# Relative bias: low parts added in DRAM and onto the mask by the transfers, instead of by GpSimd

## The chip, the cores and the metric

The kernel runs on one core of one Trainium2 chip. The metric is the device time of one execution in microseconds, the median of three runs.

## What is computed

The program runs two transformer blocks one after the other on one sequence of 256 tokens, D = 1024, all in float32 accuracy: multi-head latent attention (MLA), a squared-ReLU MLP, MoBA attention, a second MLP, then a gated delta rule mixer and a forgetting-attention mixer. The part that the change touches is the bias of MoBA. With 256 tokens there is a single block of keys, so MoBA is plain causal attention with a T5-style relative bias:

```python
def rel_bias(pq, pk):
    return table_h[h_i4, t5_bucket(pq - pk)].astype(jnp.float32)
...
lg_own = (jnp.einsum('bhqd,bhtd->bhqt', qi, k_own).astype(jnp.float32) * scale
          + rel_bias(pq4, pos_own[:, None, None, :]))
causal = (own * MOBA_BLOCK + t_ids)[None, :] <= q_idx[:, None]
parts.append(jnp.where(causal, lg_own, -jnp.inf))
```

For each of 8 heads, 256 queries and up to 256 keys the bias is one of 32 table entries, chosen by the distance of the two positions.

## The kernel before

Every projection is made of three matmuls in a reduced format (`mm3`, L171 to L173): high part times high part and the two cross products. A weight tile of 512 KB is loaded by SP into a ring of four (`load_w`, L161), ScalarE copies its high part (L164, ring of four), and VectorE, in a few places GpSimd (called POOL in the profile), subtracts to get the low part (L165, ring of four). The order of instructions on each engine is worked out before the run by a planner that follows the program's order as priority and a cost for each instruction; on the chip each engine's queue runs in that fixed order and waits on semaphores.

The bias is built beside the first MLP. `rel_bias_setup` makes the differences of neighbouring table rows as a high and a low part, side by side in one weight tile `tw` of 64 columns: rows 0 to 31 of a result come from the high parts, rows 32 to 63 from the low parts. In each of the MLP's 16 steps `rel_bias_step` multiplies `tw` with masks of "position difference reaches bucket n", and ScalarE copies the result into a staging tile `stg` (L413), which alternates between two buffers. After every second step, eight times in all, POOL issues eight transfers of 64 KB each that write the staging tile to a DRAM tensor `bias_d` (L418): four carry the high parts to `bias_d[0]`, four the low parts to `bias_d[1]`. After the MLP `rel_bias_finish` reads both halves back into SBUF with the query on the partitions: the high halves into `bias` (L422, L423), the low halves into two tiles `b2` of four heads each (L427, L428); POOL adds `b2` (L429) and then the causal mask `cmask` (L430), four tensor operations of 128x1536.

`bias` lies in the first 3072 columns of tile `bias_s`; the positions lie behind it in the same tile. It is first read in MoBA's attention, where VectorE adds it to the scaled logits (`attend`, L339). Before that MoBA norms its input: `ms_eps` and `rsqrt` (L182 to L187), a Newton iteration of small VectorE operations, and the query, key and value projections for four heads (`qkv_quad`, with `head_sumsq`, L698, and `proj_tok`).

In MLA, `rope_apply` (L476 to L479) rotates the queries of each pair of heads on POOL; the last pair's last instruction is the addition at L479. `queued(list)` makes the instructions traced inside it follow the given ones in the order of their engine.

Of the kernel before, what the change touches and what calls it, by code (L numbers as in the profile page):

```python
# [19 lines left out]
P = 128  # L20
S = 256
# [89 lines left out]
def kernel(ctx: ExitStack, tc: tile.TileContext, I: dict, out: bass.AP, small_at: dict):  # L111
# [12 lines left out]
    def slot(i, shape, dt=F32):  # L124

        return big.tile(shape, dt, tag=f"s{i}", name=f"s{i}")
# [13 lines left out]
    @contextmanager  # L140
    def queued(after):

        with ExitStack() as es:
            for i in after or ():
                es.enter_context(tc.issue_after(i))
            yield
# [131 lines left out]
    def wview(name, l=None):  # L278
        w = I[name] if l is None else I[name][l]
        return w.rearrange("(k p) n -> p k n", p=P)  # L280
# [15 lines left out]
    def out_proj(oT, w, then, between=None):  # L296

        a = [[acc_tile() for _ in range(2)] for _ in range(NT)]  # L300
        wc = []

        def group(t, ks):
            for k in ks:
                for hf in range(2):
                    mm3(a[t][hf], sl(oT, slice(None), k, slice(t * P, (t + 1) * P)),
                        sl(wc[k], slice(None), slice(hf * 512, (hf + 1) * 512)), k == 0, k == KD - 1)

        for k in range(4):
            wc += load_w(w[:, k:k + 1, :], 1, D)  # L310
            if between is None:
                for t in range(NT):
                    group(t, (k,))
            else:
                group(0, (k,))
        if between is not None:
            between()
            group(1, range(4))
        for k in range(4, KD):
            wc += load_w(w[:, k:k + 1, :], 1, D)  # L320
        for t in range(NT):
            group(t, range(4, KD))
            for hf in range(2):
                then(t, hf, a[t][hf])
# [42 lines left out]


    bias = bias_s[:, 0:3072].rearrange("p (h k) -> p h k", h=H)
    bias_d = dr.tile([2, S, H, S], F32, tag="bias_d", name="bias_d")  # L370

    def rel_bias_setup():
        pk = bias_s[:, 3072:3328]
# [23 lines left out]
    def rel_bias_step(i, pq, pk, tw):  # L397

        b, half = divmod(i, 2)
        if i == 0:  # L400
            rel["masks"] = slot(12, [P, 8, S], F32R)
            masks(0, pq, pk)
        if i < 15:
            masks(i + 1, pq, pk)
        if half == 0:
            rel["stg"] = slot(9 + b % 2, [64, 8, S])
        stg = rel["stg"]
        for g2 in (2 * half, 2 * half + 1):
            p = aux_tile()
            for j in range(2):  # L410
                T.matmul(p[0:64, j * S:(j + 1) * S], lhsT=tw[:, 0, :], rhs=rel["masks"][:, (4 * i + 2 * (g2 % 2) + j) % 8],
                         start=True, stop=True)
            A.activation(stg[:, 2 * g2:2 * g2 + 2, :], p[0:64].rearrange("p (a b) -> p a b", a=2), AF.Copy)  # L413
        if half == 1:
            for part in range(2):
                for q4 in range(4):
                    r0 = part * 32 + q4 * 8
                    nc.gpsimd.dma_start(  # L418
                        bias_d[part, 64 * q4 + 8 * b:64 * q4 + 8 * b + 8].rearrange("g h k -> h g k"), stg[r0:r0 + 8])

    def rel_bias_finish():
        nc.gpsimd.dma_start(bias[:, :, 0:128], bias_d[0, 0:128, :, 0:128])  # L422
        nc.gpsimd.dma_start(bias[:, :, 128:384], bias_d[0, 128:256])  # L423
        for h4 in range(2):
            hs = slice(4 * h4, 4 * h4 + 4)
            b2 = slot(13 + h4, [P, 4, 384])
            nc.gpsimd.dma_start(b2[:, :, 0:128], bias_d[1, 0:128, hs, 0:128])  # L427
            nc.gpsimd.dma_start(b2[:, :, 128:384], bias_d[1, 128:256, hs])  # L428
            G.tensor_tensor(bias[:, hs], bias[:, hs], b2, op=ALU.add)  # L429
            G.tensor_tensor(bias[:, hs], bias[:, hs], cmask[:, None, :].to_broadcast([P, 4, 384]), op=ALU.add)  # L430


    def rope_tables():
# [37 lines left out]
    def rope_apply(eng, dst, src, tab, nh):  # L471

        ta, tb = tab
        sh = [P, NT, nh, 32]
        t2 = w1k([P, NT, nh, ROPE])
        eng.tensor_tensor(t2[:, :, :, 0:32], src[:, :, :, 32:64], tb[:, :, None, 0:32].to_broadcast(sh), op=ALU.mult)  # L476
        eng.tensor_tensor(t2[:, :, :, 32:64], src[:, :, :, 0:32], tb[:, :, None, 32:64].to_broadcast(sh), op=ALU.mult)
        eng.tensor_tensor(dst, src, ta[:, :, None, :].to_broadcast([P, NT, nh, ROPE]), op=ALU.mult)
        eng.tensor_tensor(dst, dst, t2, op=ALU.add)  # L479

    def mla():
        hT = pair_tile(1, KD)
# [72 lines left out]
        kT = slot(6, [P, H, S])  # L555
        vt = slot(7, [P, NT, H, P])
        oT = pair_tile(3, H)
        wkv_c = []

        def heads(hp):  # L560
            wc = load_w(wq[:, :, hp * 384:(hp + 1) * 384], 3, 384, (G,) if hp == 0 else None)
# [36 lines left out]
            for dst, c0, i in ((qn, 0, 0), (kn, 192, 2)):  # L598
                V.tensor_tensor(dst, raw[:, :, :, c0:c0 + P], r6[:, :, i, :, None].to_broadcast([P, NT, 2, P]), op=ALU.mult)
            qr = w1k([P, NT, 2, ROPE])  # L600
            rope_apply(G, qr, raw[:, :, :, 128:192], tabs["q"], 2)
            V.tensor_tensor(qr, qr, r6[:, :, 1, :, None].to_broadcast([P, NT, 2, ROPE]), op=ALU.mult)
            for src, dst, g in ((qn, qT, gs[:, 0:1]), (kn, kT, gs[:, 3:4])):
                p = aux_tile()
# [23 lines left out]
        for stage, hp in ((heads, 0), (attention, 0), (heads, 1), (attention, 1), (heads, 2), (attention, 2), (heads, 3), (attention, 3)):  # L628
            stage(hp)
        out_proj(oT, wview("mla_w_o", 0), add_x)  # L630


    def mlp(l, extra=None):
# [626 lines left out]
        post_norm_out(oT, wview("fox_w_out_2", 0), "fox_post_norm_2", store)  # L1260


    mla()
    rb = rel_bias_setup()
    mlp(0, lambda f: rel_bias_step(f, *rb))
    rel_bias_finish()
# [28 lines left out]
```

## Time and profile before

| | |
|---|---|
| median of three runs | 982.36 us (981.1 to 984.11) |
| the profiled execution's own time | 988.49 us |
| its span, first to last instruction | 986.7 us |
| mean granted TensorE clock in it | 0.967 |
| HBM read, written | 147.84 MB, 5.78 MB |

The profile is one execution of its own. PE is TensorE's matmul side, PEld its weight loads, DVE is VectorE, ACT is ScalarE, POOL is GpSimd, SP the engine that only issues transfers. The tile names are those of the program, with `s` for any of the large numbered slots, so `bias`, `stg` and `b2` all read as `s`. PEclk is the granted TensorE clock as a share of the full one.

### The profile page before, as it was taken

The numbers are of one execution on the slowest core, as the hardware profiler recorded it, in microseconds if no ns is written. First come the engines' busy times: TensorE is split into PE (matmuls) and PEld (weight loads), VectorE is DVE, ScalarE is ACT, GpSimd is POOL, SyncE is SP. The second block draws the span as 40 slices with busy tenths as digits, with TensorE's granted clock in tenths as the row PEclk, the third lists the DMA queues.
The fourth block names the chain that finished last, engine by engine and source line by source line (L and its number), as shares of the span: only waits on it lengthen the run. The fifth ranks groups of instructions, "written<-read, shape, count | busy, mean of one in ns | idle before, by whom it ended". The sixth has DMA issues, their size and how long they took to land.

```text
span 986.7 us, 14702 instructions
## 1 busy us (share of the span) xinstructions
PE 911.0 (92%) x5474; PEld 790.9 (80%) x5474; DVE 649.1 (66%) x1331; ACT 519.9 (53%) x963; POOL 171.9 (17%) x205
## 2 busy tenths in 40 slices
PE   8799889999999979998999999999993897999996
PEld 8576689998988768778999989889992885789884
DVE  6897375655555875756555445678982578877775
ACT  6675354645445535645454445578652124856653
POOL 1420121111112710022000000010396303000000
PEclk9899999999999979999999999999997898999998
DMA  8344147666667645436566655355753104365431
GB/s 286 112 152 129 44 135 228 193 192 192 192 192 226 201 150 162 140 106 204 179 190 196 196 180 171 117 168 157 211 155 91 33 22 149 96 227 171 140 117 65
DMA packets 92456, 154.61 MB, mean 157 GB/s; under 512 B 9160, under 2 KB 60128, under 8 KB 92128
## 3 DMA queue, kind: packets, MB, share of 16 engines
q1 hardware_dynamic: 87072, 141.53, 45.9%
q0 software_dynamic: 5168, 12.10, 4.4%
q8 instruction: 43, 0.70, 0.3%
q14 instruction: 29, 0.24, 0.1%
q10 hardware_dynamic: 144, 0.03, 0.0%
HBM read 147.84 MB, written 5.78 MB: 156 GB/s over the span
## 4 chain that ended last, share of the span: by engine, by line
PE 40%; DMA 18%; DVE 17%; ACT 10%; issue 8%; POOL 6%; DVEq 0%; ACTq 0%; SPq 0%; POOLq 0%
DMA raw<-in_mlp_w_in_dram 14%; PE acc L171 9%; PE acc L173 9%; PE acc L172 9%; ACT whi L164 4%; DVE wlo L165 4%; DVE s L165 3%; POOL s L981 2%; POOL s L979 2%; POOL s L165 1%; PE aux L1052 1%; DVE rs_b L185 1%; DMA raw<-in_moba_w_qkv_dram 1%; ACT s L413 1%; PE aux L353 1%
## 5 line engine op out<-in xcount | busy, mean ns | idle before, releaser
L165 DVE TENSOR_TENSOR wlo<-raw,whi 128x1024 fp32r<-128x1024 f32 (+3 forms) x194 | 235.3, 1216 | 188.6 <-ACT whi L164 187.7
L164 ACT ACTIVATE whi<-raw 128x1024 fp32r<-128x1024 f32 (+3 forms) x206 | 210.3, 1025 | 220.3 <-DMA raw<-in_mlp_w_in_dram 142.6
L172 PE MATMUL acc<-wlo,s 128*128 128x512 f32 (+2 forms) x424 | 168.9, 399 | 7.4 <-DVE wlo L165 7.2
L171 PE MATMUL acc<-whi,s 128*128 128x512 f32 (+2 forms) x424 | 171.5, 408 | 4.5 <-ACT whi L164 2.5
L173 PE MATMUL acc<-whi,s 128*128 128x512 f32 (+2 forms) x424 | 167.2, 396 | 0.0
L173 PE MATMUL aux<-s,wlo 128*128 128x256 f32 (+2 forms) x528 | 149.5, 283 | 3.1 <-DVE wlo L165 3.1
L171 PE MATMUL aux<-s,whi 128*128 128x256 f32 (+2 forms) x528 | 149.4, 283 | 2.3 <-DVE s L257 2.3
L172 PE MATMUL aux<-s,whi 128*128 128x256 f32 (+2 forms) x528 | 149.3, 283 | 0.0
L171 PEld LDWEIGHTS aux<-s,whi 128*128 128x128 f32 (+2 forms) x528 | 99.6, 189 | 5.0 <-DVE s L257 2.8
L173 PEld LDWEIGHTS aux<-s,wlo 128*128 128x128 f32 (+2 forms) x528 | 99.6, 189 | 4.1 <-DVE wlo L165 3.5
L171 PE MATMUL acc<-s,w2k 128*128 128x512 f32 x256 | 100.9, 394 | 1.0 <-ACT w2k L674 1.0
L173 PE MATMUL acc<-s,w2k 128*128 128x512 f32 x256 | 101.3, 396 | 0.6 <-DVE w2k L675 0.5
L171 PEld LDWEIGHTS acc<-whi,s 128*128 128x128 f32 x424 | 82.2, 194 | 23.9 <-ACT whi L164 3.0
L172 PEld LDWEIGHTS aux<-s,whi 128*128 128x128 f32 (+2 forms) x528 | 99.6, 189 | 1.6
L172 PE MATMUL acc<-s,w2k 128*128 128x512 f32 x256 | 100.7, 393 | 0.0
L172 PEld LDWEIGHTS acc<-wlo,s 128*128 128x128 f32 x424 | 82.3, 194 | 21.3 <-DVE wlo L165 8.3
L173 PEld LDWEIGHTS acc<-whi,s 128*128 128x128 f32 x424 | 82.4, 194 | 15.5 <-DVE s L257 0.7
L173 PE MATMUL acc<-s,wlo 128*128 128x256 f32 x256 | 72.8, 285 | 1.4 <-DVE wlo L165 1.4
L165 DVE TENSOR_TENSOR s<-raw,s 128x1024 fp32r<-128x1024 f32 x60 | 70.8, 1218 | 4.9 <-ACT s L164 4.9
L172 PE MATMUL acc<-s,whi 128*128 128x256 f32 x256 | 73.0, 285 | 0.5 <-DVE s L257 0.2
L171 PE MATMUL acc<-s,whi 128*128 128x256 f32 x256 | 73.0, 285 | 0.4 <-ACT s L256 0.3
L164 ACT ACTIVATE s<-raw 128x1024 fp32r<-128x1024 f32 x64 | 64.1, 1048 | 6.3 <-DMA raw<-in_mlp_w_out_dram 6.3
(353 smaller groups left out, 1493.3 us busy)
## 6 DMA issues: line engine op xcount, KB each, us to landing
raw<-in_mlp_w_in_dram SPq DMA_DIRECT2D x64, 512.0 KB, 5.2
raw<-in_mlp_w_out_dram SPq DMA_DIRECT2D x64, 512.0 KB, 4.1
raw<-in_gdn_w_in_dram SPq DMA_DIRECT2D x32, 512.0 KB, 4.7
raw<-in_moba_w_qkv_dram SPq DMA_DIRECT2D x24, 512.0 KB, 4.1
raw<-in_fox_w_in_dram SPq DMA_DIRECT2D x16, 512.0 KB, 4.6
raw<-in_kv_w_dram SPq DMA_DIRECT2D x16, 512.0 KB, 3.9
raw<-in_mla_w_o_dram SPq DMA_DIRECT2D x8, 512.0 KB, 4.0
bias_d<-s POOLq DMA_DIRECT2D x64, 64.0 KB, 4.8
```

The costliest lines, as they stand in the source:

```text
L164: A.activation(hi[:, :k * b], rs, AF.Copy)
L165: e.tensor_tensor(lo[:, :k * b], rs, hi[:, :k * b].bitcast(F32), op=ALU.subtract)
L171: T.matmul(o, lhsT=l[0], rhs=r[0], start=start, stop=False)
L172: T.matmul(o, lhsT=l[0], rhs=r[1], start=False, stop=False)
L173: T.matmul(o, lhsT=l[1], rhs=r[0], start=False, stop=stop)
L185: V.scalar_tensor_tensor(b, dst, -0.5, x, op0=ALU.mult, op1=ALU.mult)
L353: T.transpose(pt[:, j * P:(j + 1) * P], pr[:, j * P:(j + 1) * P], ident)
L413: A.activation(stg[:, 2 * g2:2 * g2 + 2, :], p[0:64].rearrange("p (a b) -> p a b", a=2), AF.Copy)
L979: G.tensor_tensor(t3[:, 0:n, 0:c], xb[:, j, 0:c][:, None, :].to_broadcast([P, n, c]), bt[:, j, j + 1:32][:, :, None].to_broadcast([P, n, c ...
L981: G.tensor_tensor(xb[:, j + 1:32, 0:c], xb[:, j + 1:32, 0:c], t3[:, 0:n, 0:c], op=ALU.subtract)
L1052: T.matmul(px[z][:, j * P:(j + 1) * P], lhsT=a, rhs=b, start=True, stop=True)
```

## The change

The low parts are no longer kept in a DRAM half of their own. The four low-part transfers of a batch add onto the rows that the four high-part transfers of the same batch have written. A new function `rel_bias_mask` fills `bias` with the causal mask, repeated for the eight heads, by one POOL transfer from the input tensor; it is queued behind the last rope addition of MLA, which `mla` now returns. `rel_bias_finish` consists of two transfers from `bias_d` that add onto the mask in SBUF. The four POOL tensor operations and the two `b2` tiles are gone.

```diff
-    bias_d = dr.tile([2, S, H, S], F32, tag="bias_d", name="bias_d")
+    bias_d = dr.tile([S, H, S], F32, tag="bias_d", name="bias_d")
+
+    def rel_bias_mask():
+
+        nc.gpsimd.dma_start(bias, I["small"][:, None, small_at["cmask"][0]:small_at["cmask"][1]].to_broadcast([P, H, 384]))
...
             for part in range(2):
                 for q4 in range(4):
-                    r0 = part * 32 + q4 * 8
-                    nc.gpsimd.dma_start(
-                        bias_d[part, 64 * q4 + 8 * b:64 * q4 + 8 * b + 8].rearrange("g h k -> h g k"), stg[r0:r0 + 8])
+                    r0, q0 = part * 32 + q4 * 8, 64 * q4 + 8 * b
+                    nc.gpsimd.dma_start(bias_d[q0:q0 + 8].rearrange("g h k -> h g k"), stg[r0:r0 + 8],
+                                        accum_op=ALU.add if part else ALU.bypass)
 
     def rel_bias_finish():
-        nc.gpsimd.dma_start(bias[:, :, 0:128], bias_d[0, 0:128, :, 0:128])
-        nc.gpsimd.dma_start(bias[:, :, 128:384], bias_d[0, 128:256])
-        for h4 in range(2):
-            hs = slice(4 * h4, 4 * h4 + 4)
-            b2 = slot(13 + h4, [P, 4, 384])
-            nc.gpsimd.dma_start(b2[:, :, 0:128], bias_d[1, 0:128, hs, 0:128])
-            nc.gpsimd.dma_start(b2[:, :, 128:384], bias_d[1, 128:256, hs])
-            G.tensor_tensor(bias[:, hs], bias[:, hs], b2, op=ALU.add)
-            G.tensor_tensor(bias[:, hs], bias[:, hs], cmask[:, None, :].to_broadcast([P, 4, 384]), op=ALU.add)
+        nc.gpsimd.dma_start(bias[:, :, 0:128], bias_d[0:128, :, 0:128], accum_op=ALU.add)
+        nc.gpsimd.dma_start(bias[:, :, 128:384], bias_d[128:256], accum_op=ALU.add)
...
-        eng.tensor_tensor(dst, dst, t2, op=ALU.add)
+        return eng.tensor_tensor(dst, dst, t2, op=ALU.add).ins
...
-        wkv_c = []
+        wkv_c, roped = [], []
...
-            rope_apply(G, qr, raw[:, :, :, 128:192], tabs["q"], 2)
+            roped[:] = [rope_apply(G, qr, raw[:, :, :, 128:192], tabs["q"], 2)]
...
         out_proj(oT, wview("mla_w_o", 0), add_x)
+        return roped
...
-    mla()
+    with queued(mla()):
+        rel_bias_mask()
     rb = rel_bias_setup()
     mlp(0, lambda f: rel_bias_step(f, *rb))
     rel_bias_finish()
```

## Rows read from the trace of the kernel before

**Rows 1.** The page's first part: busy us, share of the span, instructions.
```profile
PE 911.0 (92%) x5474; PEld 790.9 (80%) x5474; DVE 649.1 (66%) x1331; ACT 519.9 (53%) x963; POOL 171.9 (17%) x205
```

**Rows 2.** Busy us by stage: length, PE, PEld, DVE, ACT, POOL, PEclk, DMA share, GB/s.
```profile
324.00:334.00 10.00, 10.00 (x53) 8.10 (x52) 7.12 (x21) 7.67 (x18) 4.45 (x7) 1.00 0.85 275
334.00:349.00 15.00, 9.20 (x41) 7.30 (x39) 14.86 (x9) 6.47 (x8) 14.79 (x4) 0.88 0.29 97
349.00:356.00 7.00, 5.85 (x14) 4.66 (x15) 5.21 (x6) 0.60 (x1) 0.00 (x0) 0.52 0.65 206
```

**Rows 3.** POOL's timeline, 317 to 350: start, us, engine, line, operation, idle before.
```profile
317.73 4.44 POOL L418 DMA_DIRECT2D bias_d<-s  x8 [16.34 <-ACT s L413]
323.62 0.92 POOL L422 DMA_DIRECT2D s<-bias_d  x1 [1.45 <-DMA bias_d<-s]
...
333.99 4.46 POOL L429 TENSOR_TENSOR s<-s,s 128x1536 f32<-128x1536 f32 x1 [5.55 <-DMA s<-bias_d]
...
345.53 3.42 POOL L430 TENSOR_TENSOR s<-s,small 128x1536 f32<-128x1536 f32 x1
```

**Rows 4.** VectorE's timeline, 325 to 352.
```profile
332.38 0.16 DVE L185 SCALAR_TENSOR_TENSOR rs_b<-r,mse 128x2 f32<-128x2 f32 x1
...
335.00 3.47 DVE L185 SCALAR_TENSOR_TENSOR rs_b<-r,mse 128x2 f32<-128x2 f32 x1
...
346.18 2.79 DVE L187 SCALAR_TENSOR_TENSOR r<-rs_b,r 128x2 f32<-128x2 f32 x1
348.89 2.35 DVE L165 TENSOR_TENSOR wlo<-raw,whi 128x1024 fp32r<-128x1024 f32 x2
```

**Rows 5.** TensorE's matmuls, 342 to 358.
```profile
342.59 0.39 PE L173 MATMUL acc<-whi,s 128*128 128x512 f32 x1
342.81 0.39 PE L171 MATMUL acc<-whi,s 128*128 128x512 f32 x1
350.15 0.80 PE L172 MATMUL acc<-wlo,s 128*128 128x512 f32 x1 [6.95 <-DVE wlo L165]
...
355.01 0.63 PE L171 MATMUL acc<-whi,s 128*128 128x512 f32 x1
355.44 0.52 PE L172 MATMUL acc<-wlo,s 128*128 128x512 f32 x1
```

**Rows 6.** ScalarE's timeline, 338 to 372.
```profile
355.25 0.60 ACT L697 ACTIVATE w2k<-acc 128x512 f32<-128x512 f32 x1 [11.18 <-PE acc L173]
```

**Rows 7.** POOL's timeline, 79 to 110.
```profile
80.80 0.74 POOL L479 TENSOR_TENSOR w1k<-w1k 128x256 f32<-128x256 f32 x1
105.47 2.36 POOL L165 TENSOR_TENSOR wlo<-raw,whi 128x1024 fp32r<-128x1024 f32 x1 [23.93 <-ACT whi L164]
```

**Rows 8.** Busy us by stage, columns as in the second group.
```profile
82.00:98.00 16.00, 14.15 (x67) 9.53 (x65) 10.90 (x28) 8.50 (x18) 0.00 (x0) 0.95 0.42 121
148.00:174.00 26.00, 26.00 (x172) 23.88 (x171) 16.00 (x26) 13.24 (x18) 4.78 (x8) 1.00 0.71 216
```

**Rows 9.** DMA queues from 325 to 335: packets, MB, share of 16 engines.
```profile
q0 software_dynamic: 832, 3.07, 95.0%
q1 hardware_dynamic: 2, 0.00, 0.6%
```

**Rows 10.** DMA issues of the bias: count, KB each, median us to landing.
```profile
bias_d<-s POOLq DMA_DIRECT2D x64, 64.0 KB, 4.8
...
s<-bias_d POOLq DMA_DIRECT2D x3, 512.0 KB, 7.7
```

**Rows 11.** Waits of ScalarE and TensorE, 110 to 324: us, times, longest.
```profile
ACT whi L164 <- DMA raw<-in_mlp_w_in_dram: 72.2, 17, 8.5
...
PE aux L411 <- ACT s L413: 1.8, 1, 1.8
```

**Rows 12.** VectorE's timeline, 374 to 384.
```profile
378.76 0.74 DVE L339 SCALAR_TENSOR_TENSOR w2k<-aux,r,s 128x128 f32<-128x128 f32 x2
```

**Rows 13.** TensorE's matmuls in a late head of MLA.
```profile
94.06 0.61 PE L353 MATMUL aux<-gains,w2k 128*128 128x128 f32 x3 [1.08 <-DVE w2k L349]
95.31 0.49 PE L357 MATMUL aux<-w2k,s 128*128 128x128 f32 x2 [0.64 <-ACT w2k L355]
```

## The prediction

> **What bounds the kernel now.** I read the page's first part first: TensorE is busy for 92% of the span, VectorE for 66%, POOL for 17% [rows 1]. POOL is no bound by its sum. So the question is where TensorE is not busy, and whether one of those places belongs to the relative bias. One poor slice of the span lies near 345 us, where the bias is put together, so I cut that stretch into three with the busy time by stage [rows 2]. The reader should see that from 324 to 334 TensorE is full, that from 334 to 349 it works for 9.20 us of 15 while POOL is busy for 14.79 and VectorE for 14.86, with only nine VectorE instructions, and that from 349 to 356 the granted clock is 0.52 on average.
>
> The engines' timelines then say why. POOL runs four tensor operations on 128x1536 from 333.99 to 348.95 without a break [rows 3]. VectorE's two-input operations in the reciprocal root, L185 and L187, work on two columns and take 0.16 us at 332.38; inside POOL's stretch four of them take 2.8 to 3.5 us [rows 4]. The one at 335.00 ends at 338.47, POOL's first addition at 338.45; the one at 346.18 ends at 348.97, POOL's last at 348.95. So they stand still until the running POOL instruction is over. Behind the last of them is the low part of a weight, L165, at 348.89, and TensorE waits for exactly that: its matmul at 342.81 is followed by one at 350.15, after 6.95 us put down to "DVE wlo L165" [rows 5]. The matmuls after it come 0.43 us apart up to 355.44, those before 0.22 to 0.23: the lower of the two clock levels, after the idle time.
>
> **The change, part by part.** *Removed: four POOL tensor operations.* This is the gain. TensorE's next matmul would start at 342.81 + 0.23 = 343.04 instead of 350.15: 7.1 us. The 13 matmuls from 350.15 to 355.44 would run 0.43 - 0.23 = 0.20 apart less: 2.6 us. Together 9.7 us. Would TensorE have work? ScalarE had made its high parts by 344.07 and then stood idle for 11.18 us until TensorE went on [rows 6], so only VectorE's low part was late. With the small operations at 0.16 VectorE would be through them at about 336 and free for that L165. I see no other wait in that stretch that could take its place.
>
> *Moved: the mask.* One POOL transfer of 128x8x384 floats, 1.5 MB, behind the last rope addition, which ends at 81.54; POOL then has nothing until 105.47 [rows 7]. SP's queue is not touched. The nearest price of an issue is 0.92 us [rows 3]. DMA is busy for 0.42 from 82 to 98 [rows 8]. At the 3.07 MB that POOL's queue moved in 10 us [rows 9] the transfer needs 5 us. Cost: nothing if the loads of that stretch are ahead, at most those 5 us if TensorE waits for them. The loads issued then are the MLP's first weights, whose low parts POOL makes at 105.47, so I take 0.2.
>
> *Added: 32 of the 64 staging transfers add in DRAM.* Each must wait until the plain transfer to the same rows has landed, 4.8 us after its issue in the median [rows 10]. An issue takes 4.44 / 8 = 0.56 us [rows 3]. So in each of the eight steps POOL issues four, waits 4.8 - 4 x 0.56 = 2.6 us, and issues four more. Behind the waiting instruction on POOL stands the next step's transfer only; POOL had been idle for 16.34 us before the last step's [rows 3], so the wait has cover. The staging buffer is used again two steps later. What could matter is DMA time: adding 32 x 64 KB, 2.1 MB, reads the old 2.1 MB as well. From below that costs nothing; from above, at the stage's 216 GB/s, 9.7 us if each byte held up a load that TensorE needs [rows 8]. ScalarE does wait 72.2 us in 17 waits for loads in this stage, but what reaches TensorE through ScalarE's staging copies is one wait of 1.8 us [rows 11]. That is much nearer the lower end; I take 0.5.
>
> *Changed: the finish.* Two transfers instead of six, but they add onto SBUF. The last step begins at 317.73. Its second batch then starts at about 322.5, and the finish at 322.5 + 4 x 0.56 + 4.8 = 330, or 334 if adding takes about twice as long. The price of the finish is unknown: no transfer in this trace adds. From below it is a plain one, 7.7 us [rows 10]. From above each of the two reads, reads again and writes without overlap, 3 x 7.7 us, the second after the first: 46 us. The row that it resembles most is the plain one with one more stream to read, so I take 16 us: the sum is ready at 346 to 350; before it was at 348.95. The first use is VectorE's L339 at 378.76 [rows 12], which moves up with the rest to about 369. So some 19 us are left, and this edit costs nothing. With that cover gone, each us of lateness beyond 369 costs one us, as L339 holds up the VectorE queue behind it, the low parts of weights included.
>
> The price of the addition stands on a page too. The Trainium skill, "Collectives: The Full Stack", the section on the bandwidth ceiling, says that a reduction in the DMA engines runs at half the rate of a copy because its add needs two source reads. By that rule the finish would take an estimated 15 us, and the sum would stay as it is; no row here shows an addition.
>
> **The sum.** Minus 9.7, plus 0.2, plus 0.5: minus 9.0. The profiled execution took 988.49 us with a span of 986.7; it would take 979.5. It lies 6.1 us above the median of 982.36, which comes from other runs; the waits that I remove follow from POOL's instructions and should be in those too. So 982.4 - 9.0 = 973.4.
>
> **The rivals.**
>
> *The sum comes late (slower).* If the adding transfers are as slow as the upper bound, the finish runs from 334 to 380, 11 us after 369. TensorE would wait those 11 us and lose the clock again, 2.6 us: -9.0 + 13.6 = +4.6, 987. It decides from the point where lateness and clock loss eat the gain, 6.4 us after 369, a finish of more than 41 us. Against it: 3.07 MB in 10 us on that queue for plain transfers [rows 9]. For it: nothing here shows an addition. 0.10.
>
> *The adding in the MLP takes back the gain (same).* If the 2.1 MB holds up loads byte for byte, 9.7 us: 982.6. For it: ScalarE's 72.2 us [rows 11]. Against it: from 148 to 174 TensorE is full for 26.00 of 26 us with a batch of these transfers in it [rows 8]. 0.12.
>
> *Another wait partly takes its place (faster by less).* The finish now moves its bytes from 331 to 349, beside the loads for the key and value projections. In the finish of before, POOL's queue took 95.0% of the engines' time and SP's 0.6% [rows 9]. At 343 TensorE has at most four prepared high parts, each for 12 matmuls, 4 x 12 x 0.23 = 11 us; if loads stood still until 349 and took their 4 us and two copies after that, it would miss about 4 us: 977.4. 0.08.
>
> *The planner orders differently (slower).* The order on each engine is worked out beforehand from planned costs, and the plan of POOL and of L339 changes. A head of attention with little beside it leaves TensorE idle for 1.08 + 0.64 = 1.7 us [rows 13]; if all eight MoBA heads lost their cover, 13.8 us: -9.0 + 13.8 = +4.8, 987. Against it: only the bias's own arrival changes. 0.04. A shift of 3 us either way belongs to the forecast.
>
> **How the numbers follow.** The forecast has 0.66; alone it runs from 969.5 (9.7 and some 3 us from a better order) to 977. A change under 0.3%, 2.9 us, cannot be told from none here, so "faster" ends at 979.4 and "slower" begins at 985.3. Faster: 0.66 + 0.08 = 0.74; same 0.12; slower 0.10 + 0.04 = 0.14. The range of 8 in 10 runs from 969 to 981: it takes in the third rival and most of a gain eaten in the MLP, and leaves out the two slower cases.
>
> **What would show it.** In the profile of the changed kernel L185 and L187 take 0.16 us at about 335; TensorE has no wait for L165 near 343, and its clock is 1.00 from 340 to 360. POOL shows a pause inside each batch of eight staging transfers, and after the finish nothing until the delta-rule stage. The first L339 comes near 369 and waits for no transfer. I am wrong if L339 waits for a bias transfer, if ScalarE's waits for MLP weights grow by tens of us and TensorE's with them, or if L165 is still late at 343.

## The result and the profile after

The changed kernel took 972.8 us (median of four runs, 969.1 to 977.16), against 983.16 us of the kernel before in the same session (981.1 to 984.11): a ratio of 0.989 with an interval of [0.9855, 0.9925]. The forecast was 973.4 in a range from 969 to 981, with a chance of 0.74 for faster. The profiled execution took 977.16 us with a span of 975.4 us, against 988.49 and 986.7 before.

The page's first part of the changed kernel:

```profile
PE 906.4 (93%) x5474; PEld 787.9 (81%) x5474; DVE 637.7 (65%) x1331; ACT 521.1 (53%) x963; POOL 167.1 (17%) x198
```

Against [rows 1] TensorE and VectorE execute as many instructions as before. VectorE is busy for 11.4 us less, with the same operations: that was time in which they stood still.

Busy time by stage, columns as in [rows 2] (the DMA share adds up the packets' own times, so it can pass 1):

```profile
324.00:334.00 10.00, 10.00 (x53) 8.12 (x52) 7.13 (x19) 7.67 (x18) 6.05 (x6) 1.00 0.63 67
334.00:349.00 15.00, 15.00 (x73) 12.49 (x71) 9.90 (x18) 8.74 (x12) 0.00 (x0) 1.00 1.04 261
349.00:356.00 7.00, 6.39 (x35) 5.10 (x32) 6.40 (x18) 3.28 (x5) 0.00 (x0) 1.00 0.69 210
82.00:98.00 16.00, 14.17 (x65) 9.48 (x64) 10.55 (x25) 8.08 (x18) 0.20 (x1) 0.92 0.72 228
148.00:174.00 26.00, 26.00 (x174) 23.96 (x173) 14.86 (x24) 11.91 (x15) 6.07 (x8) 1.00 0.75 222
```

The stretch from 334 to 349, where TensorE worked for 9.20 of 15 us [rows 2], is full, POOL does nothing in it, and the clock stays at its full level. The two stretches that the new transfers run beside, 82 to 98 and 148 to 174, give TensorE the same busy time as before [rows 8], with a higher DMA share.

VectorE's timeline of the changed kernel, then TensorE's waits from 324 to 434 (us in all, times, longest):

```profile
335.16 0.16 DVE L185 SCALAR_TENSOR_TENSOR rs_b<-r,mse 128x2 f32<-128x2 f32 x1
...
337.25 1.23 DVE L165 TENSOR_TENSOR wlo<-raw,whi 128x1024 fp32r<-128x1024 f32 x1 [0.40 <-ACT whi L164]
...
344.07 2.58 DVE L165 TENSOR_TENSOR wlo<-raw,whi 128x1024 fp32r<-128x1024 f32 x2 [3.16 <-ACT whi L164]
...
362.80 0.34 DVE L339 SCALAR_TENSOR_TENSOR w2k<-aux,r,s 128x128 f32<-128x128 f32 x1
```

```profile
PE aux L723 <- DVE s L716: 1.1, 2, 0.6
```

The root's operations take 0.16 us where they took 2.8 to 3.5 [rows 4], and the low parts of the weights come as soon as ScalarE has made the high ones. TensorE's wait of 6.95 us for L165 [rows 5] is gone, and no wait has taken its place: the 1.1 us that are left stood there before as 0.9.

POOL's timeline of the changed kernel (L374 is the mask, L423 the staging transfers, L427 and L428 the finish):

```profile
81.07 1.14 POOL L374 DMA_DIRECT2D s<-in_small_dram  x1
...
317.70 2.29 POOL L423 DMA_DIRECT2D bias_d<-s  x4 [13.18 <-ACT s L417]
323.47 3.61 POOL L423 DMA_DIRECT2D bias_d<-s  x4 [3.48 <-DMA bias_d<-s]
329.12 1.50 POOL L427 DMA_DIRECT2D s<-bias_d  x1 [2.05 <-DMA bias_d<-s]
330.04 2.06 POOL L428 DMA_DIRECT2D s<-bias_d  x1
424.44 1.81 POOL L983 MEMSET s<- 128x2048 f32 x1 [92.33 <-DVE w2k L339]
```

and the transfers of the bias in it (KB each, median us from issue to landing):

```profile
bias_d<-s POOLq DMA_DIRECT2D x64, 64.0 KB, 4.7
s<-in_small_dram POOLq DMA_DIRECT2D x1, 1536.0 KB, 8.7
s<-bias_d POOLq DMA_DIRECT2D x1, 1024.0 KB, 13.0
...
s<-bias_d POOLq DMA_DIRECT2D x1, 512.0 KB, 6.2
```

The second finishing transfer is issued at 330.04 and lands 13.0 us later: the sum is ready at 343.0, and its first use begins at 362.80, with 19.8 us between them. In the repeat of the same kernel it landed after 10.8 us. An adding transfer's issue costs POOL more than a plain one: 3.61 us for four, against 2.29.

**Where the gain lies.** To compare executions I cut the span at instructions that all the kernels have. "MLP" runs from POOL's first L165 after the last rope addition to the start of VectorE's residual addition at the MLP's end; "MoBA" from there to POOL's memset that opens the delta rule; "tail" from there to the span's end; "end of MLA" from the last rope addition to that first L165. The kernel before: 105.47, 322.58, 434.38 and 986.7, and the addition at 80.80 [rows 7]. All in us:

| kernel (profiled execution) | end of MLA | MLP | MoBA | tail | median, ratio to before |
|---|---|---|---|---|---|
| before | 24.7 | 217.1 | 111.8 | 552.3 | 983.16 |
| changed | 24.7 | 217.5 | 101.9 | 551.0 | 972.8, 0.989 [0.9855, 0.9925] |
| changed, again | 21.7 | 217.3 | 101.9 | 548.7 | 974.76, 0.9888 [0.9867, 0.9908] |
| four reading additions put back | 24.7 | 218.1 | 110.8 | 553.2 | 986.9, 1.0023 [1.0003, 1.0042] |
| eight memsets put in | 24.7 | 217.0 | 116.9 | 550.8 | 989.38, 1.0042 [1.0015, 1.0069] |
| three readers after the root | 21.7 | 218.3 | 103.9 | 552.8 | 978.29, 0.9932 [0.9901, 0.9964] |
| five memsets after the root | 23.3 | 215.1 | 101.9 | 551.0 | 974.62, 0.9898 [0.9866, 0.993] |
| mask on POOL, low parts by transfer | 21.7 | 217.4 | 103.8 | 550.1 | 976.38, 0.9926 [0.9899, 0.9954] |
| low parts on POOL, mask by transfer | 24.7 | 214.6 | 103.0 | 550.3 | 976.02, 0.9922 [0.9892, 0.9951] |
| before, additions on VectorE | 26.2 | 212.9 | 103.1 | 552.9 | 976.98, 0.9911 [0.9884, 0.9938] |
| mask not queued | 21.7 | 214.8 | 101.9 | 551.3 | 978.23, 0.9935 [0.9903, 0.9966] |
| low parts stored, not added | 21.7 | 216.6 | 101.8 | 550.1 | 972.61, 0.9899 [0.9866, 0.9932] |
| finish plain, no mask | 21.7 | 217.0 | 101.8 | 550.0 | 974.21, 0.9905 [0.9882, 0.9927] |
| finish four times | 21.7 | 217.5 | 23.1 more than the changed kernel, see below | | 997.78, 1.0148 [1.0121, 1.0175] |

MoBA's column is the one to read: it goes from 111.8 to 101.9, and is 101.8 or 101.9 in every run that neither holds VectorE up, nor gives it the additions, nor delays the sum. The other columns move by some us between executions, of the changed kernel too.

### The profile page after: what moved, and what is told of

Read it like the earlier page. It is cut to its first block, busy times and chain, and to the rows that moved or that the text cites. A ratio compares the mean times of both kernels' runs of the same rounds, so it can differ in the third digit from the quotient of the medians.

```text
span 975.4 us, 14708 instructions
## 1 busy us (share of the span) xinstructions
PE 906.4 (93%) x5474; PEld 787.9 (81%) x5474; DVE 637.7 (65%) x1331; ACT 521.1 (53%) x963; POOL 167.1 (17%) x198
## 4 chain that ended last, share of the span: by engine, by line
PE 55%; DMA 13%; DVE 12%; ACT 9%; POOL 6%; issue 4%; DVEq 0%; ACTq 0%; SPq 0%; POOLq 0%
PE acc L171 12%; PE acc L173 11%; PE acc L172 11%; DMA raw<-in_mlp_w_in_dram 6%; PE aux L173 3%; PE aux L171 3%; PE aux L172 3%; DVE wlo L165 3%; ACT whi L164 3%; DMA bias_d<-s 2%; POOL s L980 2%; POOL s L978 2%; DVE s L165 1%; PE aux L1051 1%; DMA raw<-in_moba_w_qkv_dram 1%
## 5 line engine op out<-in xcount | busy, mean ns | idle before, releaser
L165 DVE TENSOR_TENSOR wlo<-raw,whi 128x1024 fp32r<-128x1024 f32 (+3 forms) x194 | 235.5, 1217 | 186.5 <-ACT whi L164 185.3
L172 PE MATMUL acc<-wlo,s 128*128 128x512 f32 (+2 forms) x424 | 166.9, 394 | 0.6 <-DVE wlo L165 0.4
L171 PEld LDWEIGHTS acc<-whi,s 128*128 128x128 f32 x424 | 80.8, 191 | 23.6 <-ACT whi L164 3.0
L173 PEld LDWEIGHTS acc<-whi,s 128*128 128x128 f32 x424 | 81.0, 191 | 15.5 <-DVE s L257 0.7
L165 DVE TENSOR_TENSOR s<-raw,s 128x1024 fp32r<-128x1024 f32 x60 | 70.8, 1219 | 7.3 <-ACT s L164 7.3
L423 POOL DMA_DIRECT2D bias_d<-s x64 | 47.2, 825 | 142.7 <-ACT s L417 123.3
```

The lines of the kernel that those rows point to most:

```text
L165: e.tensor_tensor(lo[:, :k * b], rs, hi[:, :k * b].bitcast(F32), op=ALU.subtract)
L171: T.matmul(o, lhsT=l[0], rhs=r[0], start=start, stop=False)
L172: T.matmul(o, lhsT=l[0], rhs=r[1], start=False, stop=False)
L173: T.matmul(o, lhsT=l[1], rhs=r[0], start=False, stop=stop)
L423: nc.gpsimd.dma_start(bias_d[q0:q0 + 8].rearrange("g h k -> h g k"), stg[r0:r0 + 8], accum_op=ALU.add if part else ALU.bypass)
```

## The experiments

**The changed kernel again.** The same file.

> The changed kernel once more, on the chip that the other runs of this group share. Its four times before were 969.1 to 977.16 us, so this says how far they spread: expected 969 to 977, some 1.0% under the kernel before. If the lower and the higher times come from one place in the program, a profile at the other level should show it: 8 us less in one stage.

974.76 us, 10.1 below the kernel before beside it (984.84, 23 runs). MoBA's stage was 101.90, as in the first profile (101.89). The end of MLA was 2.9 us shorter; TensorE's clock accounts for that. The windows from 98 to 106 of the first and of this profile:

```profile
98.00:106.00 8.00, 6.70 (x23) 4.64 (x23) 3.09 (x8) 2.42 (x6) 0.94 (x1) 0.73 0.01 4
```

```profile
98.00:106.00 8.00, 6.69 (x37) 5.08 (x38) 3.94 (x10) 4.08 (x9) 2.35 (x1) 1.00 0.05 15
```

TensorE is as long busy with 23 matmuls at a mean clock of 0.73, part of the stretch at the lower of its two levels (1.2 of 2.4 GHz), as with 37 at 1.00. In the first profile the clock was at the lower level from 95.48 to 102.30, in the repeat not at all between the rope and the first L165; half of these 6.8 us is 3.4, enough for the 2.9. The kernel before showed 0.68 there. Of the 14 profiled executions six have 0.56 to 0.73 there and 24.7 us or more in the table's first column, eight have 0.98 to 1.00 and 21.7 to 23.3. As one kernel shows both, this is no effect of the change. The explanations below therefore go by MoBA's stage.

**The four POOL operations put back, with nothing waiting for them.** A memset and four additions of the old size, from the mask into unused tiles, behind the finish:

```diff
+        last = nc.gpsimd.dma_start(bias[:, :, 128:384], bias_d[128:256], accum_op=ALU.add)
+        cm = cmask[:, None, :].to_broadcast([P, 4, 384])
+        with tc.issue_after(last.ins):
+            d = [slot(13 + i, [P, 2048]) for i in range(2)]
+            G.memset(d[0], 0.0)
+            for i in range(4):
+                G.tensor_tensor(d[i % 2][:, 0:1536].rearrange("p (a b) -> p a b", a=4), cm, cm, op=ALU.add)
```

> The changed kernel, and behind its finish on POOL one memset (1.8 us) and four tensor operations of 128x1536 that add the mask to itself into two unused tiles, at about 334 us; nothing waits for them and the order on TensorE, VectorE and ScalarE is that of the changed kernel. Theory (VectorE's two-input operations stand still while POOL reads SBUF): the small root operations take about 3.4 us again, TensorE stands still for about 7 us near 343 at the lower clock afterwards, and the time is back at 979 to 984. Rival one (the gain came from four transfers and 1.5 MB fewer in the finish): the time stays at 969 to 977. Rival two (it came from the planner's other order of the heads): it stays at 969 to 977 too.

986.9 us: the gain is gone (1.0023), and the time lies above the 979 to 984 that I had expected. POOL's timeline, VectorE's timeline and TensorE's wait of this run:

```profile
331.58 12.01 POOL L434 TENSOR_TENSOR s<-small 128x1536 f32<-128x1536 f32 x4
```

```profile
332.57 11.05 DVE L246 TENSOR_TENSOR mse<-ss 128x2 f32<-128x2 f32 x1 [1.96 <-ACT w2k L237]
343.65 0.17 DVE L247 TENSOR_SCALAR mse<-mse 128x2 f32<-128x2 f32 x1
```

```profile
PE acc L172 <- DVE wlo L165: 7.1, 1, 7.1
```

A two-input operation on two columns stands still from 332.57 until 343.62, where POOL's last addition has ended, and TensorE waits 7.1 us for the low part behind it, as it did before (6.95) [rows 5]. All transfers are those of the changed kernel, and TensorE, VectorE, ScalarE and SP have its order. So neither fewer transfers nor another order made the gain: the POOL operations cost it, as such. One thing differs from [rows 4]: there VectorE came through at the end of single POOL operations, here it was held through all four.

**POOL operations that only write.** The same place, with eight memsets in place of the four additions:

```diff
...
+            G.memset(d[0], 0.0)
+            for i in range(8):
+                G.memset(d[i % 2], 0.0)
```

> As the run with four additions on POOL, but POOL is kept busy just as long, about 14.5 us after the first memset, by eight memsets of 128x2048, which write SBUF and read nothing. Theory (it is POOL's reading that holds VectorE): VectorE's root operations take 0.16 us, the time stays at 969 to 977. The Trainium skill, SBUF - State Buffer, Who interferes with whom, says the same: a VectorE instruction with two inputs in SBUF contends with a GpSimd instruction that reads SBUF and not with one that only writes it. Rival (any busy POOL holds VectorE): 979 to 984 as with the additions.

989.38 us, 1.0042: slower than before, so my theory that writers let VectorE pass was wrong as it stood. POOL's timeline, VectorE's, and TensorE's wait:

```profile
330.46 2.99 POOL L431 MEMSET s<- 128x2048 f32 x1
332.21 15.22 POOL L433 MEMSET s<- 128x2048 f32 x8
```

```profile
331.44 0.16 DVE L246 TENSOR_TENSOR mse<-ss 128x2 f32<-128x2 f32 x1 [1.96 <-ACT w2k L237]
331.64 15.83 DVE L247 TENSOR_SCALAR mse<-mse 128x2 f32<-128x2 f32 x1
```

```profile
PE acc L172 <- DVE wlo L165: 11.9, 1, 11.9
```

The two-input L246, the one held in the run before, takes 0.16 us inside the first memset's record. That record is no proof that it passed a memset: it is 2.99 us long, where a memset of this size takes 1.81 by itself, and it begins 1.2 us before the issue of the last finishing transfer ends (331.63), so POOL may not have been writing yet. The next operation, L247, has one tensor input and stands for 15.83 us, until the last memset is over. That memsets let two-input operations pass is shown by the next pair of runs. Taken together, the runs say that which VectorE operation is held depends on what POOL does: two inputs by readers, this single input by writers. The Trainium skill, "SBUF — State Buffer", the section on who interferes with whom, says both: a VectorE operation with two SBUF inputs contends with a GpSimd instruction that reads, not with one that only writes, and a tensor_scalar can take the shared pair of ports in a two-port mode and then contends with GpSimd. The rows of these two runs and of the next two agree with both halves.

**Readers and writers after the root.** To take L247 out of the way, a small copy from the root's result came first on POOL, and behind it three reading additions in one kernel, five memsets in the other:

```diff
...
+        with tc.issue_after(rel["last"]):
+            d = [slot(13 + i, [P, 2048]) for i in range(2)]
+            G.tensor_copy(d[0][:, 0:NT], r0)
+            cm = cmask[:, None, :].to_broadcast([P, 4, 384])
+            for i in range(3):
+                G.tensor_tensor(d[i % 2][:, 0:1536].rearrange("p (a b) -> p a b", a=4), cm, cm, op=ALU.add)
...
+            for i in range(5):
+                G.memset(d[i % 2], 0.0)
```

> The changed kernel, and behind its finish on POOL a copy that waits for the root of MoBA's norm (about 337 us) and then three additions of 128x1536 that read the mask in SBUF, 9 to 10 us; nothing waits for them, the order on TensorE, VectorE and ScalarE is that of the changed kernel. In that stretch VectorE has only operations with two inputs in SBUF (the low parts, L165) and reductions. Theory (a POOL instruction that reads SBUF holds VectorE's two-input operations, and back to back it does not let them in): the L165 that stood at 337.25 ends only at about 347, TensorE misses it from 343 on for 4 us or more and then runs at the lower clock: 5 to 8 us over the changed kernel, 978 to 984 where the kernel before is at 984. Rival (only VectorE's one-input operations are held, as in the run with memsets): no change, 972 to 976.

> As the run with three additions behind the root, but with five memsets of 128x2048 on POOL, about 9 us, which only write. In the first run with memsets VectorE's L246, a two-input operation, took 0.16 us beside a memset, and the next, L247, a tensor_scalar with one input, stood for 15.83 us until the last memset was over. Theory (memsets hold only the one-input kind): from 337 to 346 VectorE has none of these, so L165 takes 1.23 us and the time stays at 972 to 976. Rival (any busy POOL holds any VectorE operation): as with the additions, 978 to 984.

With the readers 978.29 us and a MoBA stage of 103.9; with the writers 974.62 us and 101.9, no loss at all. VectorE's timelines, first beside the readers (POOL from 334.87 to 344.99), then beside the writers (POOL from 333.04 to 341.98):

```profile
335.06 7.32 DVE L165 TENSOR_TENSOR wlo<-raw,whi 128x1024 fp32r<-128x1024 f32 x2 [0.40 <-ACT whi L164]
```

```profile
333.26 1.23 DVE L165 TENSOR_TENSOR wlo<-raw,whi 128x1024 fp32r<-128x1024 f32 x1 [0.40 <-ACT whi L164]
335.10 1.23 DVE L165 TENSOR_TENSOR wlo<-raw,whi 128x1024 fp32r<-128x1024 f32 x1 [0.62 <-ACT whi L164]
```

Two low parts take 7.32 us beside the readers and 1.23 each beside the writers. Here the engines alternated, as in [rows 4], one VectorE operation between two of POOL's. I had expected the first low part to be held until about 347 and 5 to 8 us to be lost; it ended at 338.7, and the loss was 2.0 us. TensorE had prepared tiles for most of the stall: it never waited for a low part, only 2.7 us instead of 1.1 in front of the head norms. So the time of 978.29, at the edge of what I had expected, does not confirm that expectation.

**Half of the old work on POOL.** One kernel does the mask there and the low parts by transfer, with a plain finish and no mask transfer. The other does the mask by transfer and the low parts there: all its staging transfers are plain, and the low parts are read back into the two `b2` tiles. The additions of both:

```diff
-        nc.gpsimd.dma_start(bias[:, :, 0:128], bias_d[0:128, :, 0:128], accum_op=ALU.add)
-        nc.gpsimd.dma_start(bias[:, :, 128:384], bias_d[128:256], accum_op=ALU.add)
+        nc.gpsimd.dma_start(bias[:, :, 0:128], bias_d[0:128, :, 0:128])
+        nc.gpsimd.dma_start(bias[:, :, 128:384], bias_d[128:256])
+        for h4 in range(2):
+            hs = slice(4 * h4, 4 * h4 + 4)
+            G.tensor_tensor(bias[:, hs], bias[:, hs], cmask[:, None, :].to_broadcast([P, 4, 384]), op=ALU.add)
...
+            G.tensor_tensor(bias[:, hs], bias[:, hs], b2, op=ALU.add)
```

> One part of the change alone: the low parts are added in DRAM by the transfers, the finish reads the sum with two plain transfers, and POOL adds the mask in two operations of 128x1536; no mask transfer. Theory (what counts is how long POOL holds VectorE's low part beyond 343, when TensorE needs it): the two plain transfers land at about 336 to 337, POOL runs from 337 to 344, L165 ends at about 345, TensorE misses some 2 us: 1 to 4 us over the changed kernel, 974 to 979 where the kernel before is at 984. Rival (each of the four POOL operations costs a quarter of the gain): half the gain, 978 to 980.

> The mask goes by the transfers as in the changed kernel, but the low parts stay in a DRAM half of their own and are read back into two tiles that two POOL additions of 128x1536 add at the end. The counterpart to the run that kept the mask on POOL: half of the old POOL work, started when the last transfer has landed. Theory: what costs is only POOL's tensor operations that run while VectorE has two-input work to do for TensorE. The two additions wait for the finish and the two reads (near 340 to 345), so they run later than the two mask additions of the other run (333.7 to 341.7) and hold the low parts of the weights up to about 350: MoBA's stage 103 to 108, 974 to 981. Rival: two additions are short enough for TensorE's four prepared tiles wherever they run: MoBA's stage within 1 us of 101.9, 971 to 975.

976.38 and 976.02 us; MoBA 103.8 and 103.0. Half of POOL's work costs 1.9 or 1.1 us, not half of 9.9. TensorE's wait in the first, and its first matmul after a pause in the second:

```profile
PE acc L172 <- DVE wlo L165: 1.6, 1, 1.6
```

```profile
353.05 0.41 PE L728 MATMUL aux<-gains,s 128*128 128x128 f32 x2 [1.77 <-DVE s L721]
```

In both runs POOL's two additions ran earlier than I had expected, from 333.74 to 341.68 in the first and from 335.39 to 343.56 in the second. In the second TensorE missed no low part, and the delay came out as 1.77 us in front of the head norms. Its 103.0 lies on the border between what the theory and the rival gave; it does not tell them apart. Both runs fit the reading that the stall counts only beyond what TensorE has prepared.

**The four additions on VectorE.** The kernel before, with no adding transfer at all:

```diff
-            G.tensor_tensor(bias[:, hs], bias[:, hs], b2, op=ALU.add)
-            G.tensor_tensor(bias[:, hs], bias[:, hs], cmask[:, None, :].to_broadcast([P, 4, 384]), op=ALU.add)
+            V.tensor_tensor(bias[:, hs], bias[:, hs], b2, op=ALU.add)
+            V.tensor_tensor(bias[:, hs], bias[:, hs], cmask[:, None, :].to_broadcast([P, 4, 384]), op=ALU.add)
```

> The kernel before, with its two additions and two mask additions on VectorE instead of POOL; the transfers are those of before. Theory (only the stall of VectorE behind POOL cost time): VectorE gets about 4 x 1.7 = 7 us of work, placed by the planner between 334 and 379; POOL no longer holds it. Before, VectorE was idle or held for most of that stretch, so most of the gain should come without any addition in the transfers: 973 to 978. Rival (the gain needs the fewer transfers): 980 to 985.

976.98 us, 0.9911; MoBA 103.1. VectorE's timeline, two of the four:

```profile
361.24 1.75 DVE L429 TENSOR_TENSOR s<-s,s 128x1536 f32<-128x1536 f32 x1
363.03 1.76 DVE L430 TENSOR_TENSOR s<-s,small 128x1536 f32<-128x1536 f32 x1
```

VectorE needs 1.75 us where POOL took 3.4 to 4.5 [rows 3], and the planner put the additions just ahead of their use. Of the 9.9 us in MoBA's stage 8.7 (111.8 - 103.1) come without any adding transfer: it was enough to take the work off POOL.

**The staging transfers without the addition.** All 64 plain, the low parts in a DRAM half that is never added, which leaves the low parts of the bias out:

```diff
-    bias_d = dr.tile([S, H, S], F32, tag="bias_d", name="bias_d")
+    bias_d = dr.tile([2, S, H, S], F32, tag="bias_d", name="bias_d")
...
+                    nc.gpsimd.dma_start(bias_d[part, q0:q0 + 8].rearrange("g h k -> h g k"), stg[r0:r0 + 8])
...
```

> The changed kernel with the 32 low-part staging transfers plain, into a DRAM half of their own that is never added (the low parts of the bias are left out of the result). The order on TensorE, VectorE and ScalarE is that of the changed kernel. Theory: adding in DRAM beside the MLP costs next to nothing. The pauses of 1.6 to 3.5 us between four and four staging transfers on POOL disappear (a plain one waits for the staging tile alone), the MLP's stretch takes 213 to 219 us as in the other runs, MoBA's stage stays at 102, 972 to 977. Rival: the old 2.1 MB that the additions read again hold up the MLP's loads byte for byte; then without them the MLP's stretch is 5 to 10 us shorter than 217, 963 to 968, and ScalarE's 72 us of waits for the MLP's weights fall by tens of us.

972.61 us, like the changed kernel. The MLP's stretch took 216.6 us, against 217.5 and 217.3 with the addition. POOL's last batch and ScalarE's first wait from 110 to 324:

```profile
314.24 4.44 POOL L423 DMA_DIRECT2D bias_d<-s  x8 [16.22 <-ACT s L417]
320.01 1.53 POOL L426 DMA_DIRECT2D s<-bias_d  x1 [1.33 <-DMA bias_d<-s]
```

```profile
ACT whi L164 <- DMA raw<-in_mlp_w_in_dram: 71.9, 17, 8.6
```

The pause inside the batch is gone, and ScalarE's wait for weights is much what it was with the addition (71.9 and, in the repeat, 65.1) and before (72.2) [rows 11]. The whole table says less than this pair: the four kernels whose staging transfers are all plain took 212.9 to 217.1 us in the MLP, 215.3 in the mean, the ten executions that add took 214.8 to 218.3, 217.0 in the mean. So adding in DRAM beside the MLP costs between nothing and some 2 us, which these executions do not tell from the spread; the rival wanted 5 to 10.

**The finish plain, no mask.** The mask is left out of the result:

```diff
+        nc.gpsimd.dma_start(bias[:, :, 0:128], bias_d[0:128, :, 0:128])
+        nc.gpsimd.dma_start(bias[:, :, 128:384], bias_d[128:256])
...
-    with queued(mla()):
-        rel_bias_mask()
+    mla()
```

> The changed kernel with both finishing transfers plain and without the mask's transfer (the causal mask is left out of the result). Theory: the plain transfers land sooner, 512 KB some 5 us and 1 MB some 7 to 8 us after issue instead of 6.2 and 13.0, so the addition onto SBUF makes the finish some 6 us longer, and nobody notices, because the first use stands 20 us later: MoBA's stage stays at 102 us, first L339 near 363, 972 to 977. Rival: the adding transfer takes DMA time from the loads of the key and value projections; then MoBA's stage falls by 1 to 3 us, 970 to 973.

974.21 us; MoBA 101.8. The DMA issues of this run:

```profile
s<-bias_d POOLq DMA_DIRECT2D x1, 1024.0 KB, 7.5
...
s<-bias_d POOLq DMA_DIRECT2D x1, 512.0 KB, 4.5
```

From the first issue to the last landing this plain finish takes 327.91 + 7.5 - 326.11 = 9.3 us, and the plain one of the run with the mask on POOL 10.1. The adding one took 13.9 us in the first profile of the changed kernel, and 11.8 to 14.7 in the eight profiled executions that have it and no other read of the bias beside it. Its 512 KB landed after 6.1 to 6.6 us there, plain ones after 4.5 and 4.6; its 1 MB after 10.8 to 13.8, plain ones after 7.5 and 8.4. So adding onto SBUF makes the finish some 2 to 5 us longer, and nothing in MoBA's stage notices. The end of MLA takes 21.7 us without the mask's transfer, as it does with it in the repeat (102.37 - 80.63): the mask costs nothing.

**The finish four times.** Each pair of transfers behind the one before, so that the bias is added four times:

```diff
+        for _ in range(4):
+            nc.gpsimd.dma_start(bias[:, :, 0:128], bias_d[0:128, :, 0:128], accum_op=ALU.add)
+            nc.gpsimd.dma_start(bias[:, :, 128:384], bias_d[128:256], accum_op=ALU.add)
```

> The changed kernel with the finish done four times over, each pair of transfers behind the one before (the bias is added four times, so the result holds it fourfold). Theory: the finish's time is hidden up to the first use and no further. Four finishes of about 14 us from 329 make the sum ready at about 385; VectorE's first L339 stood at 363 in the changed kernel (its planned place here may be a few us later, near 369), so it waits 16 to 22 us on the DMA queue, TensorE stands idle for about as long and its clock falls for some 3 us after it: MoBA's stage 118 to 127 instead of 102, 988 to 1000. This is the slower rival of the prediction made true: from the point of lateness each us costs one. Rival: the projections still to come cover it (planner or queue slack), MoBA's stage at most 106, 972 to 980.

997.78 us, 1.0148: the slower rival made true. VectorE's timeline, TensorE's after the pause, and the busy time by stage:

```profile
380.10 0.35 DVE L339 SCALAR_TENSOR_TENSOR w2k<-aux,r,s 128x128 f32<-128x128 f32 x1 [6.70 <-DMA s<-bias_d]
...
385.56 0.48 DVE L339 SCALAR_TENSOR_TENSOR w2k<-aux,r,s 128x256 f32<-128x256 f32 x1 [2.06 <-DMA s<-bias_d]
```

```profile
388.72 0.48 PE L353 MATMUL aux<-gains,w2k 128*128 128x128 f32 x1 [8.65 <-DVE w2k L349]
```

```profile
370.00:380.00 10.00, 10.00 (x45) 8.01 (x43) 2.45 (x2) 1.84 (x3) 1.44 (x1) 1.00 1.19 291
380.00:390.00 10.00, 1.35 (x6) 1.10 (x6) 5.40 (x10) 3.93 (x7) 0.00 (x0) 0.67 0.78 177
390.00:400.00 10.00, 10.00 (x44) 8.23 (x42) 4.28 (x11) 4.36 (x9) 0.00 (x0) 0.82 0.37 109
```

The wait itself is smaller than I had expected, 6.70 and 2.06 us in place of 16 to 22, because the planner counts the longer finish and puts L339 later: VectorE reaches it at 373.4. The projection matmuls that it draws forward for that are missing as cover later. POOL's opening memset stands elsewhere in this order, so I compare by the residual addition of MoBA's output (L328): it comes 130.7 us after the MLP's end, against 107.6 in the changed kernel (430.16 - 322.55). The two L339 come 20.2 and 25.1 us later after the MLP's end than there; the stage pays 23.1 us. TensorE's waits in it are 16.2 us in all, against 1.1; the other 8 go with the lower clock of the stretches above and with heads that lack cover, which I did not separate.

**The mask at the program's start.** Not queued behind the rope addition; the planner then put it at 1.31:

```diff
-    with queued(mla()):
-        rel_bias_mask()
+    mla()
+    rel_bias_mask()
```

> The changed kernel without the queueing of the mask transfer: the planner puts it behind POOL's first memset, within the first 2 us, the rest is in the same order. Theory (a transfer costs time only where loads are waited for): in the first 24 us the DMA engines are busy for 0.84 and TensorE waits for the first weights, so 1.5 MB more delay the start by up to 5 us: 3 to 6 us over the changed kernel, 976 to 980. Rival (the place of the mask transfer does not matter): 972 to 976.

978.23 us, 0.9935, with an interval that overlaps the repeat's. Against the two profiles of the changed kernel POOL runs 2.4 to 3.4 us late from 24 to 31 us, but only 0.2 to 0.7 us late by 46 to 56; MoBA's stage is 101.9 and the span 970.5. Inconclusive: the profile shows no place for a cost of more than 0.7 us, but it is that of the fastest of five runs (972.23, the others 975.39 to 978.83), and what those lost is not shown.

## Why the prediction was right

*The POOL operations removed.* The sum had 9.7 us, 7.1 of stall and 2.6 of clock; MoBA's stage gave 9.9, twice. Putting the readers back took 8.9 of them away again (110.8). The clock stayed at 1.00 from 324 to 356, and ScalarE, which had stood idle for 11.18 us [rows 6], worked on (8.74 us busy from 334 to 349 and 3.28 from 349 to 356, against 6.47 and 0.60 [rows 2]).

*The mask.* 0.2 predicted, nothing measured (21.7 us with and without). Its transfer took 8.7 us, longer than the 5 that I derived from the queue's rate, and beside loads that were ahead this did not matter.

*Adding in the MLP.* 0.5 predicted; the stretch beside the MLP shows nothing that stands out of its spread, so the runs confirm that the cost is small, but not its size. The pauses inside the batches were 1.6 to 3.5 us, predicted 2.6, and covered by POOL's idle time. The rival "adding takes back the gain" (0.12) is excluded: without the additions the MLP was 0.7 to 0.9 us shorter in the same order of instructions, 1.7 between the means of all executions, not 9.7.

*The finish.* Predicted to begin at 330 and to take 16 us; it began at 329.1 and took 13.9 (11.8 to 14.7 in eight executions). The sum was ready at 343.0 rather than at 346 to 350. The first use came at 362.8 rather than 369. The order of TensorE, VectorE and ScalarE is that of the kernel before up to there and differs behind it, so the planner drew the use forward; that it did so because it counts a shorter finish fits the run with four finishes, where it put the use later. That the predicted margin of some 19 us came out (19.8) is luck: both ends came early, the sum by 3 to 7 us and the use by 6. The rule of the Trainium skill that a reducing transfer runs at half the rate of a copy ("Collectives: The Full Stack", the section on the bandwidth ceiling) gave an estimate of 15 us; the page states it for the reducing step of a ring of cores, not for a transfer within one. The measured finish is 1.2 to 1.6 times the plain one (11.8 to 14.7 against 9.3 and 10.1), and single transfers 1.3 to 1.8 times. So the rule is somewhat high here and right in kind.

*The rivals.* "The sum comes late" (0.10) would have needed a finish of over 41 us; the run with four finishes shows that its price per us was judged rightly: 23.1 us for 20 to 25 us of lateness, clock included. "Another wait takes its place" (0.08) did not happen: from 334 to 349 the loads ran beside the finish at 261 GB/s of traffic and TensorE was full. "The planner orders differently" did happen, from the first use of the bias on, at no cost that shows in MoBA's stage.

*The sum.* -9.0 predicted, -10.4 and -10.1 between medians. The span of the two profiles fell by 11.3: 9.9 in MoBA's stage, 1.4 in the tail, which varies by more than that between executions of the changed kernel (548.7 and 551.0), and the other parts cancel. What was too small was the net gain: the mask's 0.2 did not appear, the adding's 0.5 cannot be told from the spread, and the stall was worth 0.2 more. The rest is no more than medians move: the interval of the ratio runs from -7.4 to -14.3 us and takes in the -9.0.

*The step that was incomplete.* "They stand still until the running POOL instruction is over" held in the trace of before, but it is not the rule: VectorE stood through four POOL additions in one run and through eight memsets in another, and alternated in a third. For the prediction it made no difference, as all of POOL's operations went. Whoever had priced the removal of one of several would have erred: half of them cost 1.1 to 1.9 of 9.9 us. What decides whether POOL lets VectorE in between two operations is open; the runs only show both. The records differ in one thing. In the two runs that held VectorE throughout, POOL's operations came straight behind its transfer issues, and each record begins about 1.2 us before the one ahead of it ends (the additions at 331.58 and 334.29, each 3.9 us long). Where the engines alternated, POOL came out of a wait, and each record begins within 0.1 us of the end of the one ahead. No run varies this by itself, so it is not shown to be the cause.

## What to carry to other kernels

An engine that is busy for a sixth of the span can still cost the whole kernel 1%, through what it holds: look for operations on a few columns that take microseconds, and see whose instruction ends when they do. A big GpSimd operation belongs where VectorE has nothing urgent, or off GpSimd; on VectorE it took half the time here and kept most of the gain. A transfer can do an addition at little cost as long as its result has slack: here the addition made the finish some 2 to 5 us longer, under a slack of 19.8. Since the price of lateness was about one for one, the slack is the number to work out first.

## What the runs showed of the hardware

- A VectorE operation on two columns, L247 with one tensor input, stood for 15.83 us beside memsets on POOL, while two-input ones of 128x1024 took 1.23 us beside memsets, their usual time; beside reading additions a two-input one on two columns stood for 11.05 us.
- VectorE was held through several POOL operations in a row (four, eight) in two runs, and let in after each in the kernel before and in another run (two L165 in 7.32 us).
- An adding transfer from DRAM onto SBUF landed after 10.8 to 13.8 us for 1 MB and 6.1 to 6.6 us for 512 KB in eight executions, where plain ones in the same place took 7.5 and 8.4, and 4.5 and 4.6, in two; the issue of one that adds in DRAM took POOL 0.9 us (3.61 for four), of a plain one 0.57 (2.29 for four).
- TensorE's mean clock from 98 to 106 was 0.56 to 0.73 in six profiled executions and 0.98 to 1.00 in eight, with the same kernel in both groups; it was worth 2.9 us between the two executions of the changed kernel.
